# A fourth couple of FFN chunks by seven block products, in three of four FFN stages of a decoder trunk

## The chip, the cores and the metric

The kernel runs on 1 core of a Trainium2 chip. The metric is the time of one execution on the device in microseconds (us), the median of several. Every time below is in us unless it is marked ns. PE is TensorE, DVE is VectorE, ACT is ScalarE, POOL is GpSimd; SP issues the loads, and POOL issues those that add to what lies in the buffer.

## The reference

Two layers, each with an FFN, a mixer and a second FFN on 256 tokens of width 1024; the FFN has 2816 inner columns. So there are four FFN stages and two mixers, in the order FFN, mixer, FFN, FFN, mixer, FFN.

```python
def rms_norm(x, g):
    xf = x.astype(jnp.float32)
    y = xf * lax.rsqrt(jnp.mean(xf * xf, axis=-1, keepdims=True) + EPS)
    return (y * g.astype(jnp.float32)).astype(x.dtype)

def swiglu(h, wi, wo):
    gate, up = jnp.split(h @ wi, 2, axis=-1)
    return (jax.nn.silu(gate) * up) @ wo
...
    for l in range(DEPTH):
        h = rms_norm(x, ffn1_pre_g[l])
        x = x + 0.5 * rms_norm(swiglu(h, ffn1_wi[l], ffn1_wo[l]), ffn1_post_g[l])
        h = rms_norm(x, mix_pre_g[l])
        y = hybrid_mixer(h, w_in[l], a_ln_g[l], a_ln_b[l], a_ws[l], a_bs[l],
                         w_pa[l], w_pb[l], w_pc[l], w_o[l])
        x = x + rms_norm(y, mix_post_g[l])
        h = rms_norm(x, ffn2_pre_g[l])
        x = x + 0.5 * rms_norm(swiglu(h, ffn2_wi[l], ffn2_wo[l]), ffn2_post_g[l])
```

The mixer is not touched by the change.

## The kernel before, in words

**Tiles.** The 256 tokens are two tiles of 128. The inner columns are 11 chunks of 256 (numbered 0 to 10), each with its gate and its up columns, so that one chunk's first product is 512 columns wide. Weights are fp32 and are worked on in two parts: `hi`, a cast by ACT (L231), and `lo`, what the cast left over, by a subtraction on DVE (L232). The tokens are split in the same way (`hh`, `hl`). Each product is three matmuls (`mm3`, L391 to L395: hi by hi, hi by lo, lo by hi). A chunk's first product for one token tile is eight steps over the width 1024, so 24 matmuls of 512 columns.

**Weights.** They come in units of 1 MB. A generator (`loader`, from L161) issues the loads in a fixed order, `plan` (from L127), on SP's queue: a wait of one load holds all that stand behind it. A unit goes into one of two buffers `raw`; `splitter` (from L223) makes hi and lo of each half unit, into rings of eight, or into buffers with the tag `q4` (nine of 128x1024) for units named in `place`. The `q4` buffers are shared with the mixer's large tiles, with the token sums, with `wa` and `wb` below, and, in a stage that follows a mixer, with the halves of chunk 0's units.

**Couples of chunks.** `QUADS = (4, 6, 8)`: chunks 4 and 5, 6 and 7, 8 and 9 are taken in couples by `pair7` (from L525), which makes the 2 by 2 blocks (two chunks, two token tiles, the width in two halves) by seven block products instead of eight (12 matmuls each). For that it needs token sums, four tiles `s1` to `s4` for the whole stage (`sums`, L487 to L514: twelve operations of 128x512 on DVE, four casts on ACT), and weight sums for each couple. Those are `wa`, `wb` and `wf`: DVE makes `wf` by L240 and L245, and POOL issues loads that add to what is in `wb` (L184) and in `wa` (L241). In the plan a couple is `B11`, `T2`, a wo unit, `B21`, `T3`, `T1`, a wo unit, `T4`, `B22`; the names stand for the weight blocks and sums in the order in which they are split. Of a couple's results, `u2` and `u3` are kept (L545) and added to or subtracted from later ones.

**Order in a stage.** Chunks 0 and 1 come first for both token tiles: in the first FFN tile by tile for each chunk, in the other three (0, tile 0), (1, tile 0), (0, tile 1), (1, tile 1). Then `sums` starts; chunks 2 and 3 are taken in the plain way, each after a unit of the second weight `wo` (products `acc`); then come the three couples, and chunk 10. The stage's start overlaps the end of the stage before: the norm of the second token tile (`prenorm`, from L344: two squares on ACT, `rs` on POOL, `xn` on DVE, transposes on PE) is worked out while PE does the first tile's products.

**Who sets the order.** The program is emitted by coroutines along a clock of estimates (`Clock`), and a list scheduler then sets the order of each engine's instructions; operations marked `high_priority` come earlier. Each engine works through its own list in order. What the scheduler made of both programs is shown with the change.

Of the kernel before, what the change touches and what calls it, by code (L numbers as in the profile page):

```python
# [24 lines left out]
EPS = 1e-6  # L25
NEG = -1.0e30
UNITS = 106
QUADS = (4, 6, 8)

NOSYNC = mybir.DependencyInfo(mybir.DependencyClass.NoSync, mybir.DependencyReason.DATA)  # L30
HOT = 60
# [7 lines left out]

class Flag:  # L40
    on = False


class Clock:
# [33 lines left out]
def trunk(ctx, tc, x, wpk, gains, lnp, wst, bst, consts, out, depth=DEPTH):  # L78
    nc = tc.nc
    V, S, G, T = nc.vector, nc.scalar, nc.gpsimd, nc.tensor  # L80
    ck = Clock()
# [44 lines left out]

    plan = []  # L127
    for l in range(depth):
        for st0, qj in ((0, QUADS), (33, None), (73, QUADS)):
            b = UNITS * l + st0  # L130
            if qj is None:
                plan += [("w", b + i) for i in range(40)]
                continue

            def c(j, q):
                return b + (2 * j if j < 2 else 3 * j - 1 if j < NCH - 1 else 28) + q

            def w(j):
                return b + (4 + 3 * j if j < NCH - 3 else j + 22)

            plan += [("w", c(j, q)) for j in range(2) for q in range(2)]
            for j in range(2, NCH - 1, 2):
                if j in qj:
                    k = Quad({}, c(j, 0), c(j, 1), c(j + 1, 0), c(j + 1, 1))
                    if j != qj[0]:
                        k.ffn, k.prev, last.next, k.par = last.ffn, last, k, 1 - last.par
                    else:
                        k.prev, k.par = None, 0
                    k.next = None
                    last = k  # L150
                    plan += [("B11", k), ("T2", k), ("w", w(j - 2)), ("B21", k), ("T3", k), ("T1", k),
                             ("w", w(j - 1)), ("T4", k), ("B22", k)]
                else:
                    for i in (j, j + 1):
                        plan += [("w", w(i - 2)), ("w", c(i, 0)), ("w", c(i, 1))]
            plan += [("w", c(NCH - 1, q)) for q in range(2)] + [("w", w(NCH - 3 + i)) for i in range(3)]
    NI = len(plan)
    WQ = (slice(0, 1024), slice(1024, 2048))
    done, raw = set(), {}

    def loader():  # L161

# [45 lines left out]
    def ready(n, kind, k):  # L208
        if kind[0] == "T":
            raw[n] = k.b if kind == "T3" else k.ffn["a" if kind == "T1" else "f"]  # L210
        return n in raw

    def splitter():
        for n, (kind, k) in enumerate(plan):
            while not ready(n, kind, k):
                next(ld)
            halves[n] = []
            for q in range(2):
                gate = place.get(n)
                while st_["free"] <= 0 if gate is None else not gate.on:  # L220
                    yield 0.2
                    gate = place.get(n)
                if gate is not None:  # L223
                    h = sp.tile([P, 1024], F32R, tag="q4", name=f"hi{n}_{q}", bufs=9)
                    lo = sp.tile([P, 1024], F32R, tag="q4", name=f"lo{n}_{q}", bufs=9)
                else:
                    st_["free"] -= 1
                    h = rp.tile([P, 1024], F32R, tag="hi", name=f"hi{n}_{q}", bufs=RING)
                    lo = rp.tile([P, 1024], F32R, tag="lo", name=f"lo{n}_{q}", bufs=RING)
                r = raw[n][q]  # L230
                S.copy(h, r)  # L231
                V.tensor_sub(lo, r, f32(h))  # L232
                halves[n].append((h, lo))
                yield 1.2
            if kind == "B11":
                f = k.ffn
                if "f" not in f:
                    f["f"] = [sp.tile([P, 1024], F32, tag="xn", name=nm("wf"), bufs=2) for _ in WQ]
                for q, c in enumerate(WQ):
                    V.tensor_add(f["f"][q], f["a"][q], k.b[q])  # L240
                    nc.gpsimd.dma_start(f["a"][q], wpk[k.u12][:, c], accum_op=ALU.add)  # L241
                    yield 0.6
            elif kind == "B21":
                for q in range(2):
                    V.tensor_add(k.ffn["f"][q], k.ffn["f"][q], raw[n][q])  # L245
                    yield 0.6
            elif kind == "T1":
                k.t1 = True
            done.add(n)
            for _ in range(3):  # L250
                next(ld, None)
# [92 lines left out]
    def prenorm(tt, gi, flag, st=None):  # L344

        xn = sp.tile([P, DM], F32, tag="xn", name=nm("xn"), bufs=2)
        st = sp.tile([P, 2], F32, tag="ss", name=nm("ss"), bufs=4)
        for i, h in enumerate(HF):
            with tc.high_priority(offset=HOT):
                q = S.activation(xn[:, h], xs[tt][:, h], AF.Square, scale=DM ** -0.5, accum_out=st[:, i:i + 1])  # L350
                if gi == 0 and tt == 1:
                    tc.add_manual_dep(q.ins, lasthi[0].ins.name, NOSYNC, reason="first tile first")
            if i == 0:
                yield 0.6
        r = rstd_of(st[:, 0:1], st[:, 1:2])
        yield 1.7
        gn = gain(gi)
        with tc.high_priority(offset=HOT):
            for h in HF:
                V.scalar_tensor_tensor(xn[:, h], xs[tt][:, h], r, gn[:, h], op0=ALU.mult, op1=ALU.mult)  # L360
        yield 1.0
        for i, h in enumerate(HF):
            to_T(xn[:, h], tt, 4 * i, 4, hh, hl)
            yield 0.7
        flag.on = True

    def post_half(acc, yn, st, i, gi, mul):

# [62 lines left out]
        ck.tick()  # L431


    def ffn(gi, nxt, first):
        acc = [None, None]
        gT, gf = {}, {}
        always = Flag()
        always.on = True
        for i in (32 + 3 * len(QUADS), 33 + 3 * len(QUADS)):
            place[st_["pos"] + i] = always  # L440

        def wi(us, j, tt, rel):
# [82 lines left out]
        def pair7(j, ss):  # L525
# [26 lines left out]
            def chunk(jj, tt, a, b, op):  # L552
# [24 lines left out]
        ss = []  # L577
        ua, ub = take(2), take(2)
        order = ((ua, 0, 0), (ua, 0, 1), (ub, 1, 0), (ub, 1, 1)) if first else \
                ((ua, 0, 0), (ub, 1, 0), (ua, 0, 1), (ub, 1, 1))  # L580
        for w, j, tt in order:
            wi(w, j, tt, tt == 1)
        ck.start(sums(ss), 0.2)
        for j in range(2, NCH - 1):
            if j == 4:
                if first:
                    load_consts()
                gain(gi + 1)
                gain(gi + 2)
            if j // 2 * 2 in QUADS:  # L590
                if j % 2 == 0:
                    pair7(j, ss)
                continue
            uo = take(1)[0]
            wo(uo, j - 2, 0, False)
            wo(uo, j - 2, 1, True)
            us = take(2)
            wi(us, j, 0, False)
            wi(us, j, 1, True)
# [334 lines left out]
        T.matmul(warm[:, 0:P], ident, ident, start=True, stop=True)  # L934
    for l in range(depth):
        b = 6 * l
        ffn(b, b + 2, l == 0)
        mixer(l, b + 2, b + 4)
        ffn(b + 4, b + 6 if l + 1 < depth else None, False)
    while ck.ev:  # L940
        ck.until(lambda: not ck.ev)

# [96 lines left out]
```

## Time and profile before

| what | us |
|---|---|
| median of 3 runs | 1259.87 (1258.27 to 1259.88) |
| the profiled execution's own time | 1260.91 |
| its span in the profile | 1259.2 |
| PE busy in it | 1240.5 (99%) |
| DVE busy | 949.3 (75%) |
| ACT busy | 729.5 (58%) |
| POOL busy | 75.5 (6%) |

By the products on PE the second FFN stage goes from 456.5 to 637.3, the third from 637.3 to 818, the fourth from 1074.5 to 1252.6. The stage in which the change is followed here is the second: chunks 0 and 1 from 456.5 to 480.9, chunks 2 and 3 with two wo units to about 514.6, and three couples of about 31 us each to 607.

A line of the trace's timeline gives start, duration, engine, source line, operation, the tile written and the tiles read, and in brackets how long the engine sat idle before it and what it waited for. DVE's and PE's durations overlap with the next instruction; the distance of two starts is what an instruction takes in a row of such.

### The profile page before, as it was taken

What the parts mean: (1) busy time and instruction counts of PE and PEld (TensorE: products, weight loads), DVE (VectorE), ACT (ScalarE), POOL (GpSimd) and SP (SyncE); (2) the same over time, 40 slices, a digit from 0 to 9 for tenths busy, and PEclk for the clock granted to TensorE, in tenths of its full rate; (3) what the DMA queues carried; (4) which work ended last, traced back from release to release, by engine and by line L of the source; (5) the groups of instructions that cost most, each with busy time, mean ns of one, the idle gap of its engine ahead of it and who ended that gap; (6) DMA issues with size and microseconds to landing.
All of it is one profiled execution on the core that took longest, in us unless ns stands there. A gap on an engine that the chain in (4) does not pass through costs nothing.

```text
span 1259.2 us, 16367 instructions
## 1 busy us (share of the span) xinstructions
PE 1240.5 (99%) x6284; PEld 1029.3 (82%) x6284; DVE 949.3 (75%) x1185; ACT 729.5 (58%) x996; POOL 75.5 (6%) x129
## 2 busy tenths in 40 slices
PE   8999999999999999999999999999999999999997
PEld 6777878998778878888878888789977788888886
DVE  5889977645765877899768899865467668689983
ACT  5566656435656465666645666654366655557652
POOL 0001001000000010010011010010000000110000
PEclk8999999999999999999999999999999999999999
DMA  7899555554435557885668785744543455687851
GB/s 251 279 316 264 172 201 194 188 212 166 136 134 178 192 167 271 261 270 167 239 207 260 252 258 185 236 175 161 210 181 119 149 173 200 213 240 250 250 195 65
DMA packets 45294, 259.41 MB, mean 206 GB/s; under 512 B 5280, under 2 KB 5408, under 8 KB 21280
## 3 DMA queue, kind: packets, MB, share of 16 engines
q1 hardware_dynamic: 38304, 233.20, 52.0%
q0 software_dynamic: 6912, 25.17, 10.5%
q8 instruction: 49, 0.80, 0.3%
q14 instruction: 29, 0.24, 0.1%
HBM read 257.30 MB, written 1.05 MB: 205 GB/s over the span
## 4 chain that ended last, share of the span: by engine, by line
PE 82%; DMA 6%; DVE 6%; ACT 3%; issue 1%; POOL 1%; SPq 0%; DVEq 0%; POOLq 0%; ACTq 0%
PE mm L392 15%; PE mm L394 15%; PE mm L393 15%; DMA raw<-wpk 5%; PE acc L394 5%; PE acc L393 5%; PE acc L392 5%; DVE lo L232 3%; PE qk L393 3%; PE qk L394 3%; PE qk L392 3%; PE tr L339 2%; ACT hi L231 2%; PE pj L394 1%; PE pj L392 1%; PE pj L393 1%
## 5 line engine op out<-in xcount | busy, mean ns | idle before, releaser
L232 DVE TENSOR_TENSOR lo<-raw,hi 128x1024 fp32r<-128x1024 f32 x376 | 451.8, 1220 | 153.2 <-ACT hi L231 148.1
L231 ACT CAST hi<-raw 128x1024 fp32r<-128x1024 f32 x376 | 387.2, 1050 | 259.4 <-DMA raw<-wpk 78.6
L392 PE MATMUL mm<-hi,hh 128*128 128x512 f32 x784 | 314.0, 401 | 1.7 <-ACT hh L332 1.7
L394 PE MATMUL mm<-hi,hl 128*128 128x512 f32 x784 | 307.3, 392 | 0.2 <-DVE hl L333 0.2
L393 PE MATMUL mm<-lo,hh 128*128 128x512 f32 x784 | 306.8, 391 | 0.0
L392 PEld LDWEIGHTS mm<-hi,hh 128*128 128x128 f32 x784 | 147.9, 189 | 33.3 <-issue 2.7
L394 PEld LDWEIGHTS mm<-hi,hl 128*128 128x128 f32 x784 | 147.7, 188 | 32.7 <-DVE hl L333 0.9
L393 PEld LDWEIGHTS mm<-lo,hh 128*128 128x128 f32 x784 | 148.1, 189 | 27.9
L392 PE MATMUL acc<-hi,gT 128*128 128x512 f32 x352 | 139.3, 396 | 0.2 <-ACT gT L332 0.2
L394 PE MATMUL acc<-hi,gT 128*128 128x512 f32 x352 | 137.6, 391 | 0.3 <-DVE gT L333 0.3
L393 PE MATMUL acc<-lo,gT 128*128 128x512 f32 x352 | 137.7, 391 | 0.0
L392 PE MATMUL qk<-hh,hi 128*128 128x256 f32 x320 | 91.2, 285 | 0.0
L394 PE MATMUL qk<-hh,lo 128*128 128x256 f32 x320 | 90.5, 283 | 0.0
L393 PE MATMUL qk<-hl,hi 128*128 128x256 f32 x320 | 90.5, 283 | 0.0
L392 PE MATMUL mm<-hi,sA 128*128 128x512 f32 x192 | 77.2, 402 | 0.8 <-DVE sg L479 0.8
L394 PEld LDWEIGHTS acc<-hi,gT 128*128 128x128 f32 x352 | 66.1, 188 | 14.3 <-DVE gT L333 0.8
L392 PEld LDWEIGHTS acc<-hi,gT 128*128 128x128 f32 x352 | 66.1, 188 | 13.5 <-ACT gT L332 0.7
L393 PEld LDWEIGHTS acc<-lo,gT 128*128 128x128 f32 x352 | 66.2, 188 | 13.0
L394 PE MATMUL mm<-hi,sA 128*128 128x512 f32 x192 | 75.1, 391 | 0.0
L393 PE MATMUL mm<-lo,sA 128*128 128x512 f32 x192 | 74.9, 390 | 0.0
L332 ACT CAST gT<-tr 128x256 fp32r<-128x256 f32 x88 | 32.5, 369 | 63.6 <-PE tr L339 63.5
L393 PEld LDWEIGHTS qk<-hl,hi 128*128 128x128 f32 x320 | 61.4, 192 | 0.1
(170 smaller groups left out, 1724.2 us busy)
## 6 DMA issues: line engine op xcount, KB each, us to landing
raw<-wpk SPq DMA_DIRECT2D x187, 1024.0 KB, 4.9
wb<-wpk SPq DMA_DIRECT2D x24, 512.0 KB, 7.0
wb<-wpk POOLq DMA_DIRECT2D x24, 512.0 KB, 9.2
wa<-wpk SPq DMA_DIRECT2D x24, 512.0 KB, 6.0
wa<-wpk POOLq DMA_DIRECT2D x24, 512.0 KB, 9.5
gain<-gains SPq DMA_DIRECT2D x12, 512.0 KB, 7.7
x<-x SPq DMA_DIRECT2D x2, 512.0 KB, 5.6
raw<-wpk SPq DMA_DIRECT2D x2, 512.0 KB, 6.5
```

The lines of the kernel that those rows point to most:

```text
L231: S.copy(h, r)
L232: V.tensor_sub(lo, r, f32(h))
L332: lasthi[0] = S.copy(h_out, src)
L339: T.transpose(tr[:, k * P:(k + 1) * P], src[:, k * P:(k + 1) * P], ident)
L392: T.matmul(o, ah, bh, start=first, stop=False, skip_group_check=go_on)
L393: T.matmul(o, ah, bl, start=False, stop=False, skip_group_check=go_on)
L394: T.matmul(o, al, bh, start=False, stop=stop, skip_group_check=go_on)
```

## The change

Chunks 2 and 3 become a fourth couple in the second, third and fourth FFN stage; the first stage keeps three. The parity of the `wb` buffers is counted from the last couple on, so that the new couple's second `wb` tile takes the tag `shl`. The first couple's B11 is split only once the second token tile's norm is emitted (`normed`). `sums` starts after the third of the four first products instead of after the fourth. The gains are loaded at chunk 3 instead of 4.

```diff
-QUADS = (4, 6, 8)
+FOUR = (1, 2, 3)
...
+def quads(i):
+
+    return (2, 4, 6, 8) if i in FOUR else (4, 6, 8)
...
-        for st0, qj in ((0, QUADS), (33, None), (73, QUADS)):
+        for st0, qj in ((0, quads(2 * l)), (33, None), (73, quads(2 * l + 1))):
...
+                    k.par, k.gate = qj[::-1].index(j) % 2, 2 * l + st0 // 73 if j == 2 else None
                     if j != qj[0]:
-                        k.ffn, k.prev, last.next, k.par = last.ffn, last, k, 1 - last.par
+                        k.ffn, k.prev, last.next = last.ffn, last, k
                     else:
-                        k.prev, k.par = None, 0
+                        k.prev = None
...
             if kind == "B11":
                 f = k.ffn
+                while k.gate is not None and k.gate not in normed:
+                    yield 0.2
...
         flag.on = True
+        if tt == 1:
+            normed.add({0: 0, 4: 1, 6: 2, 10: 3}.get(gi))
...
-    def ffn(gi, nxt, first):
+    def ffn(gi, nxt, idx):
+        first, qj = idx == 0, quads(idx)
...
-        for w, j, tt in order:
+        for i, (w, j, tt) in enumerate(order):
             wi(w, j, tt, tt == 1)
-        ck.start(sums(ss), 0.2)
+            if i == (3 if first else 2):
+                ck.start(sums(ss), 0.2)
         for j in range(2, NCH - 1):
-            if j == 4:
+            if j == (4 if first else 3):
...
-            if j // 2 * 2 in QUADS:
+            if j // 2 * 2 in qj:
```

PE's list has 5815 rows before and 5779 after the change: 36 rows fewer, which are 36 matmuls of 512 columns. The lists are the same up to the first mixer's end; from there they differ in the places shown.

SP's queue, around the start of the second FFN stage. raw73 to raw76 are the units of chunks 0 and 1, raw77 is the first wo unit in the new program and raw79 the unit B21; in the program before, raw77 is the first wo unit too, and raw78 and raw79 are chunk 2. Before:

```order
L115 DMA raw73_3729<-wpk 128x2048
L115 DMA raw74_3765<-wpk 128x2048
L115 DMA raw75_3794<-wpk 128x2048
L115 DMA raw76_3816<-wpk 128x2048
L115 DMA raw77_3877<-wpk 128x2048
L115 DMA raw78_3905<-wpk 128x2048
L115 DMA wb_307_3907<-wpk 128x1024
L115 DMA wb_308_3908<-wpk 128x1024
L115 DMA raw79_3952<-wpk 128x2048
L115 DMA raw80_3986<-wpk 128x2048
```

With the change:

```order
L120 DMA wb_289_3666<-wpk 128x1024
L120 DMA wb_290_3667<-wpk 128x1024
L120 DMA raw73_3735<-wpk 128x2048
L120 DMA raw74_3771<-wpk 128x2048
L120 DMA raw75_3800<-wpk 128x2048
L120 DMA raw76_3822<-wpk 128x2048
L120 DMA wa_299_3824<-wpk 128x1024
L120 DMA wa_300_3825<-wpk 128x1024
L120 DMA raw77_3887<-wpk 128x2048
L120 DMA raw79_3915<-wpk 128x2048
L120 DMA wb_311_3917<-wpk 128x1024
L120 DMA wb_312_3918<-wpk 128x1024
```

`wb`, the weights to which POOL adds, is loaded ahead of the four units of chunks 0 and 1; the two loads of `wa` stand behind these, and raw77 behind `wa`. POOL's list moves in the same way: its two accumulating loads of `wb` stood between the two norms' `rs`, and stand ahead of all four now.

DVE, second FFN stage, from the transposed result of chunk 0's first tile on (`gT`, `sg` are the results of chunks; `sA` are the token sums). Before:

```order
L333 TENSOR_TENSOR gT_320_4007<-tr_325_4049,gT_320_4007 128x256
L452 TENSOR_TENSOR sg_328_4062<-mm_321_4008,sg_328_4062 128x256
L333 TENSOR_TENSOR gT_326_4057<-tr_329_4077,gT_326_4057 128x256
L452 TENSOR_TENSOR sg_331_4095<-mm_327_4058,sg_331_4095 128x256
L232 TENSOR_TENSOR lo88_0_4105<-raw79_3952,hi88_0_4104 128x1024
L232 TENSOR_TENSOR lo88_1_4120<-raw79_3952,hi88_1_4119 128x1024
L333 TENSOR_TENSOR gT_320_4007<-tr_332_4114,gT_320_4007 128x256
L491 TENSOR_TENSOR sA_336_4146<-hh_94,hl_95 128x512
L232 TENSOR_TENSOR lo89_0_4132<-raw80_3986,hi89_0_4131 128x1024
L452 TENSOR_TENSOR sg_335_4143<-mm_330_4091,sg_335_4143 128x256
L491 TENSOR_TENSOR sA_337_4148<-hh_94,hl_95 128x512
L232 TENSOR_TENSOR lo89_1_4151<-raw80_3986,hi89_1_4150 128x1024
```

With the change:

```order
L341 TENSOR_TENSOR gT_324_4005<-tr_329_4047,gT_324_4005 128x256
L463 TENSOR_TENSOR sg_334_4066<-mm_325_4006,sg_334_4066 128x256
L341 TENSOR_TENSOR gT_332_4061<-tr_335_4089,gT_332_4061 128x256
L248 TENSOR_TENSOR wf_330_4052<-wa_299_3824,wb_289_3666 128x1024
L238 TENSOR_TENSOR lo86_0_3924<-wa_299_3824,hi86_0_3923 128x1024
L248 TENSOR_TENSOR wf_331_4053<-wa_300_3825,wb_290_3667 128x1024
L238 TENSOR_TENSOR lo86_1_3943<-wa_300_3825,hi86_1_3942 128x1024
L238 TENSOR_TENSOR lo87_0_4070<-wf_330_4052,hi87_0_4069 128x1024
L238 TENSOR_TENSOR lo87_1_4080<-wf_331_4053,hi87_1_4079 128x1024
L463 TENSOR_TENSOR sg_337_4107<-mm_333_4062,sg_337_4107 128x256
L502 TENSOR_TENSOR sA_338_4110<-hh_94,hl_95 128x512
L502 TENSOR_TENSOR sA_339_4112<-hh_94,hl_95 128x512
```

Before, the product `sg` of chunk 0's second tile (mm_327) stood right behind the first tile's `gT`; now six operations of 128x1024 on `wa` and `wb` stand ahead of that product (mm_333 here), and the first token sums behind it.

PE, second FFN stage, where chunk 1's second tile ends (mm_336) and the first couple begins (mm_350), with the change:

```order
L402 MATMUL mm_336_4103<-hi85_1_3903,hh_94 128x512
L403 MATMUL mm_336_4103<-lo85_1_3904,hh_94 128x512
L404 MATMUL mm_336_4103<-hi85_1_3903,hl_95 128x512
L402 MATMUL acc_352_4231<-hi88_0_4120,gT_324_4005 128x512
L402 MATMUL acc_353_4232<-hi88_0_4120,gT_324_4005 128x512
L347 MATMUL tr_342_4136<-ident_73,sg_337_4107 128x128 x2
L402 MATMUL mm_350_4191<-hi86_0_3923,hh_94 128x512
L403 MATMUL mm_350_4191<-lo86_0_3924,hh_94 128x512
```

The transposes of that `sg` (tr_342) stand two matmuls behind the last product of chunk 1.

PE, where T3's product ends (into mm_351 or mm_368) and T1's begins, with the change: first in the new couple, then in the next one:

```order
L403 MATMUL mm_351_4192<-lo90_1_4214,sA_345_4173 128x512
L404 MATMUL mm_351_4192<-hi90_1_4213,sA_345_4173 128x512
L402 MATMUL mm_358_4316<-hi91_0_4223,sA_340_4128 128x512
...
L402 MATMUL mm_368_4449<-hi99_1_4496,sA_345_4173 128x512
L403 MATMUL mm_368_4449<-lo99_1_4497,sA_345_4173 128x512
L404 MATMUL mm_368_4449<-hi99_1_4496,sA_345_4173 128x512
L402 MATMUL acc_352_4231<-hi101_0_4535,gT_361_4350 128x512
L402 MATMUL acc_353_4232<-hi101_0_4535,gT_361_4350 128x512
L402 MATMUL acc_354_4251<-hi101_0_4535,gT_361_4350 128x512
L402 MATMUL acc_355_4252<-hi101_0_4535,gT_361_4350 128x512
L402 MATMUL mm_373_4589<-hi100_0_4507,sA_340_4128 128x512
```

The tile into which T1 goes (mm_358, mm_373) takes the PSUM buffer of T3's, which DVE's `u3` reads (L556 now, L545 before). Before, T1's product followed T3's directly as well, into the buffer of an earlier product, which DVE had read (L479) before.

## Rows read from the trace of the kernel before

**Rows 1.** The page, busy time of each engine over the span (share of the span, instructions).

```profile
PE 1240.5 (99%) x6284; PEld 1029.3 (82%) x6284; DVE 949.3 (75%) x1185; ACT 729.5 (58%) x996; POOL 75.5 (6%) x129
```

**Rows 2.** Windows, one middle couple of the second FFN stage; busy us, instructions, PEclk, DMA share, GB/s.

```profile
545.00:575.90 30.90, 30.90 (x141) 25.38 (x140) 30.60 (x37) 21.73 (x28) 2.59 (x3) 1.00 0.87 256
```

**Rows 3.** Timeline of PE, the stage's first wo product, and the next product, both ends.

```profile
480.71 0.39 PE L392 MATMUL acc<-hi,gT 128*128 128x512 f32 x1
486.39 0.39 PE L392 MATMUL mm<-hi,hh 128*128 128x512 f32 x1
...
494.78 0.39 PE L393 MATMUL mm<-lo,hh 128*128 128x512 f32 x1
```

**Rows 4.** Chain of waits, second FFN stage, the second token tile's norm.

```profile
462.51 0.95 POOL wb L184
464.52 0.76 DVE xn L360
465.42 0.63 PE tr L339 x4
```

**Rows 5.** Timeline of SP's queue, starts of the second and the fourth FFN stage.

```profile
456.11 14.87 SPq L115 DMA_DIRECT2D wb<-wpk  x2
1073.29 14.88 SPq L115 DMA_DIRECT2D wb<-wpk  x2
```

**Rows 6.** DMA, the load issued at 470.66 (the second wb): KB, us to landing.

```profile
wb<-wpk SPq DMA_DIRECT2D x1, 512.0 KB, 4.6
```

**Rows 7.** Timeline of DVE, second FFN stage.

```profile
473.57 0.42 DVE L333 TENSOR_TENSOR gT<-tr,gT 128x256 fp32r<-128x256 f32 x1 [3.16 <-ACT gT L332]
475.70 0.42 DVE L452 TENSOR_TENSOR sg<-mm,sg 128x256 f32<-128x256 f32 x1 [1.70 <-ACT sg L451]
...
481.53 0.68 DVE L491 TENSOR_TENSOR sA<-hh,hl 128x512 f32<-128x512 f32 x1
482.13 1.22 DVE L232 TENSOR_TENSOR lo<-raw,hi 128x1024 fp32r<-128x1024 f32 x1
483.26 0.42 DVE L452 TENSOR_TENSOR sg<-mm,sg 128x256 f32<-128x256 f32 x1
483.60 0.68 DVE L491 TENSOR_TENSOR sA<-hh,hl 128x512 f32<-128x512 f32 x1
...
501.30 1.21 DVE L240 TENSOR_TENSOR wf<-wa,wb 128x1024 f32<-128x1024 f32 x1
502.43 0.41 DVE L333 TENSOR_TENSOR gT<-tr,gT 128x256 fp32r<-128x256 f32 x1
```

**Rows 8.** Page and DMA: a 1 MB load's landing, all; then those issued at 72.8, 106.5.

```profile
raw<-wpk SPq DMA_DIRECT2D x187, 1024.0 KB, 4.9
raw<-wpk SPq DMA_DIRECT2D x1, 1024.0 KB, 8.5
raw<-wpk SPq DMA_DIRECT2D x1, 1024.0 KB, 11.0
```

**Rows 9.** Timelines of ACT and PE, third FFN stage, the second token tile's norm.

```profile
640.10 1.05 ACT L231 CAST hi<-raw 128x1024 fp32r<-128x1024 f32 x1
642.51 0.63 ACT L350 ACTIVATE xn<-x 128x512 f32<-128x512 f32 x1 [1.36 <-DVE x L382]
646.02 0.63 PE L339 MATMUL tr<-ident,xn 128*128 128x128 f32 x4 [0.44 <-DVE xn L360]
```

**Rows 10.** Timelines of PE and DVE, a block product's last matmul and its reader.

```profile
533.65 0.39 PE L394 MATMUL mm<-hi,sA 128*128 128x512 f32 x1
534.08 0.69 DVE L545 TENSOR_TENSOR cc<-mm,u 128x512 f32<-128x512 f32 x1
```

**Rows 11.** Timeline of PE and windows, the program's start.

```profile
10.66 0.79 PE L392 MATMUL mm<-hi,hh 128*128 128x512 f32 x1 [1.66 <-ACT hh L332]
10.00:14.00 4.00, 3.18 (x7) 2.08 (x8) 3.12 (x5) 3.52 (x9) 0.88 (x2) 0.50 0.88 303
18.00:20.00 2.00, 2.00 (x10) 1.65 (x9) 1.55 (x3) 1.98 (x4) 0.00 (x0) 1.00 0.82 254
```

More of the change, by code (lines that the diff above doesn't have):

```diff
@@ L158, in trunk @@
     WQ = (slice(0, 1024), slice(1024, 2048))
-    done, raw = set(), {}
+    done, raw, normed = set(), {}, set()
     def loader():
@@ L438, in ffn @@
         always.on = True
-        for i in (32 + 3 * len(QUADS), 33 + 3 * len(QUADS)):
+        for i in (32 + 3 * len(qj), 33 + 3 * len(qj)):
             place[st_["pos"] + i] = always
@@ L936, in trunk @@
         b = 6 * l
-        ffn(b, b + 2, l == 0)
+        ffn(b, b + 2, 2 * l)
         mixer(l, b + 2, b + 4)
-        ffn(b + 4, b + 6 if l + 1 < depth else None, False)
+        ffn(b + 4, b + 6 if l + 1 < depth else None, 2 * l + 1)
     while ck.ev:
```

## The prediction

> **What bounds the kernel now.** I read the page's busy times first: PE is busy 99% of the span, DVE 75% [rows 1], so the sum of PE's matmuls is the time, and a matmul less is a gain only while nothing else ends last. Next the windows by stage: in a middle couple DVE is busy 30.60 of 30.90 [rows 2]; PE and DVE are nearly equal there, and DVE keeps up only because it comes to a couple ahead of PE. Next PE's timeline for the price of a matmul: from 486.39 to 494.78 there are 37 starts [rows 3], 0.2268 each. Last the chain of waits and the queues at the start of a stage, where the change moves the most: PE waits there for the second tile's norm [rows 4], and a load of wb waits at the head of SP's queue [rows 5]. DVE idles in that place, 3.16 and 1.70 ahead of two results [rows 7]: it is the time in which DVE could work ahead, and the question is whether the change can use it.
>
> **What the change removes.** Two plain chunks for two tiles are 4 x 24 = 96 matmuls, a couple is 7 x 12 = 84. Twelve fewer in three stages are 36, as the order has it: 36 x 0.2268 = **8.2**. In the second stage POOL's issue of an accumulating load (0.95, at 462.51) lies in the chain to the second tile's norm, and PE's transposes wait at 465.42 [rows 4]. It now stands ahead of the norms. PE's next start came about 0.7 late there; I take **0.7** off (0 to 0.7), once only: in the fourth stage PE did not wait at that place. The gains' loads, moved by one chunk, have one answer, nothing: they wait at no engine in the rows that I read.
>
> **What it adds on DVE.** A couple splits 18 half units and adds wf four times, 22 operations of 128x1024, where two plain chunks have 12. Rates on DVE, by starts in a row: 128x1024 1.13 (482.13 to 483.26, 501.30 to 502.43), 128x512 0.60, 128x256 0.34 [rows 7]. The question is when they run.
>
> *The first couple, after a mixer (second and fourth stage).* All times here are the trace's own; what moves PE moves them together. The first load of wa needs the q4 buffer for which the second wb waited: SP stood at it from 456.11 on, and it was issued at 470.66, when PE had used chunk 0's first half for the second tile [rows 5, 6]. It landed after 4.6 [rows 6]; so wa is there at 475.3. In DVE's new order six operations on wa and wf stand ahead of sg of the second tile: 6 x 1.13 + 0.42 = 7.2, so sg is ready at 482.5. PE wants it for its transposes at about 481.3, two matmuls behind the last of chunk 1 (480.71 was the first wo matmul [rows 3]). From there to the last split that T2's product needs, by the order, DVE has five operations of 128x1024, eight of 128x512 and three of 128x256: 5.7 + 4.8 + 1.0 = 11.5, which is 494.0. PE has 44 matmuls and two couples of transposes (0.23 each) from 480.71 to T2: 10.5, so it would be there at 491.2. T2's last matmul is 17 starts on, at 497.9, and u2, which reads its product, can start 0.43 later (a reader started so long after its product's last matmul [rows 10]). After u2 (0.6) DVE has four operations of 128x1024, one of 128x512 and u3: 4.5 + 0.6 + 0.7, so u3 is done at 504.7. T1's product waits for u3, since it goes into the buffer that u3 reads. From 480.71 to T1 PE has 76 matmuls and the two couples of transposes: 17.2 + 0.5 = 17.7, so it would be there at 498.4. It waits **6.3** in all, in two or three pieces; without the wait of DVE for T2, 4.9. DVE does not use the idle time of 470 to 475: nothing in its order ahead of wa can run there, and the sums, which could, stand behind.
>
> *The next wo unit.* Its load is issued when lo of the first one is split, at about 487.5 (482.5 and five of DVE's operations more), behind accumulations that POOL issues from 477.6 on (as lo of wa's first half is done). PE wants its cast (1.05 [rows 9]) six matmuls into T2, at 495.4, so a landing up to 6.8 after the issue costs nothing. A 1 MB load lands after 4.9 in the median; two that were issued with accumulations under way took 8.5 and 11.0 [rows 8], which would cost 1.7 and 4.2. I take half of the smaller, **0.8**, since part of the accumulations has landed by then. So 7.1 a stage, 14.2 for two; bounds 4.9 and 10.5 a stage if the order of DVE decides, and nothing if its idle time could be used.
>
> *The third stage* follows an FFN, and wa's buffers come free with the last products of the stage before; DVE has its six operations done before the second tile. But ACT's casts of wa now stand ahead of the square of the second tile (642.51), behind which the transposes at 646.02 already wait [rows 9]. A cast is 1.05 [rows 9]: 0 to 1.05, I take **0.55**.
>
> *u3 in every couple.* In all couples of these stages T1's product now waits for u3, before for an earlier read. DVE starts on a product 0.43 after its last matmul did (533.65 to 534.08 [rows 10]) and needs 0.68; PE has 0.23 and, by the order, four wo matmuls, 0.91, to fill it. With DVE free, that is even: 1.11 against 1.14. With one 128x1024 operation in the way it is 1.1 to 1.2 late, and DVE is busy 99% of such a couple [rows 2]. I take 0.2 for each of the ten couples not counted above (0 to 1.2): **2.0** (0 to 12).
>
> **The sum**: -8.2 - 0.7 + 14.2 + 0.55 + 2.0 = +7.9. The profiled execution took 1260.91, 1.04 above the median of 1259.87; its time would become 1268.8, and against the median I forecast **1267.5**. A measurement of this kernel can tell about 0.2%, 2.5, from no change.
>
> **A rule against the change.** At the program's start PE sat 1.66 without work before 10.66, after only transposes, and the granted clock from 10 to 14 was 0.50, the lower of the two levels (1.2 GHz); it was back at 1.00 from 18 on [rows 11]. Waits of PE inside stages, such as that at 465.42, left it at 1.00. The Trainium skill (TensorE: Matmul & The Clock Gate, "HAM oscillation — how this bites in real kernels") says that PE's idle gaps between matmuls throttle the clock again; if the new waits came in long pieces, the clock would fall in them. My sum holds it at 1.00; the time with a fall, from rows, is rival 4's 1273.5.
>
> **The rivals.**
> 1. *DVE's work is done ahead* (faster). If wa landed 6 earlier, or DVE came to its sums in its idle time, PE would not wait for u3, and 8.2 + 0.7 would remain: 1252 on the profiled time, 1251 against the median. For it: DVE is idle 23% of its time as a whole, and 3.16 and 1.70 just there [rows 7]. Against: each engine keeps its order, wa's load waits on PE, and the point at which this decides is that DVE, which has u3 ready 29.4 after wa lands, would have to have it ready within the 23.1 from 475.3 to PE's arrival at 498.4. Chance 0.2, with the cases in which part of it holds.
> 2. *It evens out* (same). The waits of the first couple come at their lower bound (4.9 twice), because DVE loses nothing on T2 and the wo unit lands in time, and the later couples and the third stage cost nothing: -8.9 + 9.8 = +0.9, 1261 against the median. For it: T1's price is even with DVE free. Against: three things must all go well. Chance 0.15.
> 3. *DVE paces all couples* (much slower). One 128x1024 operation stands ahead of u3 in most of the ten couples, at 1.2 each, which adds up to 10 to the forecast: 1277. For it: 30.60 of 30.90 [rows 2], and no lead left after the first couple. Against: the order often has u3 placed early. Chance 0.12.
> 4. *The clock falls* in the waits of the second and fourth stage. At the lower level, seen from 10 to beyond 14, PE loses half of its work; six at that level cost 3, twice 6 in all: 1273.5. Against: 1.00 in all later waits. Chance 0.08.
> That the change does not do what it says is left out: the order has 36 rows fewer.
>
> **How the numbers follow.** My forecast has 0.45, with a range of its own of 1263 (the first couple's lower bound with the other terms) to 1273 (its upper bound in one stage and half of it in the other). Slower by over 0.2% is that with rivals 3 and 4: 0.65; same is rival 2, 0.15; faster is rival 1, 0.2. The whole range reaches from 1253, inside rival 1's lesser forms, to 1275; it leaves out about half of rival 1 and of rival 3, 0.16.
>
> **What would show it.** PE has 36 matmuls fewer. SP's loads of wa start at about 470, their casts at 475; sg of the second tile on DVE at about 482, u3 at 503 to 506, and PE's waits from 481 to 506 and in the fourth stage's like place name DVE's sums, sg and u, or ACT's hi, 4.9 to 10.5 together. The wait at 465 is gone. In the later couples PE waits at T1 for DVE's u (L556). It is wrong if PE waits for under 2 in the first couple, if DVE's idle time around 473 shrinks to nothing, or if the later couples take 30.9 or less each.

## The result, and the profile after

The changed kernel takes **1311.07** in the median of 5 runs (1304.79 to 1313.52), the kernel before 1259.87 on the same chip; the ratio is 1.0392, 95% interval 1.0364 to 1.0420. So it is slower by 49 to 51, where the forecast was 7.6. The profiled execution is the fastest of the five: 1304.79, span 1303.1, which is 43.9 above the span before.

The page of the changed kernel, busy times (as [rows 1]) and the DMA queues (q0 carries POOL's accumulating loads; its row before stands last; columns: packets, MB, share of the 16 DMA engines' span):

```profile
PE 1247.8 (96%) x6248; PEld 1024.3 (79%) x6248; DVE 990.0 (76%) x1230; ACT 738.6 (57%) x1017; POOL 84.6 (6%) x141
...
q1 hardware_dynamic: 39168, 233.20, 49.7%
q0 software_dynamic: 8640, 31.46, 13.1%
...
q0 software_dynamic: 6912, 25.17, 10.5%
```

PE has its 36 matmuls fewer (6248 against 6284), but more time passes in them. q0 has grown from 25.17 MB to 31.46 MB. What PE waited for, in the changed kernel (engine and line that waited, what for: us in total, times, longest):

```profile
PE tr L347 <- DVE xn L368: 13.5, 7, 3.6
PE tr L347 <- DVE cc L490: 9.7, 9, 2.2
PE acc L402 <- ACT hi L237: 9.0, 5, 3.7
PE tr L347 <- DVE sg L463: 4.5, 6, 1.2
PE mm L402 <- DVE u L556: 3.5, 4, 1.4
```

Before, the first of these was 3.3, the second 0.5, and there was no row for `acc` behind `hi` or for `u`. The largest wait is one that I had priced as a gain: the norm (`xn`). The chain of waits of the changed kernel at the end of the first mixer, where the first token tile of the second FFN stage is normed:

```profile
435.15 9.57 DMA raw<-wpk
444.80 1.06 ACT hi L237
445.88 2.36 DVE lo L238 x2
448.24 0.66 DVE yn L383 x2
...
453.90 0.76 DVE xn L368
454.80 0.72 PE tr L347 x4
455.52 0.43 PE wo L402
```

A 1 MB load takes 9.57. Behind it, on ACT and DVE, stand the operations of the norm, in the order of each engine; PE waits 3.63 for its transposes at 454.80, and the matmul after that takes 0.43 and not 0.23. POOL's timeline shows what ran beside that load: the two accumulating loads of the new couple's `wb`, moved to this place by the change.

```profile
430.92 0.95 POOL L190 DMA_DIRECT2D wb<-wpk  x1 [82.16 <-PE pj L404]
432.22 0.86 POOL L190 DMA_DIRECT2D wb<-wpk  x1 [0.35 <-issue]
```

The first couple of the second stage, in DVE's timeline and PE's (what answers to [rows 7] and [rows 3]):

```profile
477.59 1.23 DVE L248 TENSOR_TENSOR wf<-wa,wb 128x1024 f32<-128x1024 f32 x1 [0.78 <-DMA wa<-wpk]
...
484.41 0.42 DVE L463 TENSOR_TENSOR sg<-mm,sg 128x256 f32<-128x256 f32 x1
...
504.45 0.69 DVE L556 TENSOR_TENSOR u<-mm,u 128x512 f32<-128x512 f32 x1 [4.85 <-PE mm L404]
...
510.20 0.68 DVE L556 TENSOR_TENSOR u<-mm,u 128x512 f32<-128x512 f32 x1
```

```profile
500.02 1.22 PE L402 MATMUL acc<-hi,gT 128*128 128x512 f32 x2 [3.33 <-ACT hi L237]
501.04 0.63 PE L404 MATMUL mm<-hi,sA 128*128 128x512 f32 x1
...
510.94 0.50 PE L402 MATMUL mm<-hi,sA 128*128 128x512 f32 x1 [1.45 <-DVE u L556]
```

sg is done 7.2 after the start of wf, as worked out. At 500.02 PE waits for the next wo unit's cast; that load was issued at 489.90 and took 8.9. DVE, whose next operation is u2, waits 4.85 for T2's product. Then u2, u3 and T1 follow, T1 0.06 after u3's end.

Windows of the changed kernel (columns as [rows 2]): behind the two waits of over 3 in the second stage, then behind a wait of 2.21 at 745.32 in the third, then the second and third couple of the second stage:

```profile
454.80:458.00 3.20, 3.20 (x11) 2.52 (x12) 3.20 (x4) 0.86 (x2) 0.00 (x0) 0.56 0.00 0
500.60:503.00 2.40, 2.40 (x7) 1.90 (x6) 0.00 (x0) 0.61 (x3) 0.00 (x0) 0.50 0.93 386
745.30:748.70 3.40, 3.38 (x9) 2.81 (x10) 3.32 (x5) 0.79 (x2) 0.00 (x0) 0.51 0.94 378
518.60:550.40 31.80, 31.23 (x142) 25.45 (x141) 28.79 (x33) 20.31 (x27) 3.43 (x4) 1.00 0.95 298
550.40:585.00 34.60, 31.55 (x142) 25.34 (x141) 31.88 (x37) 20.76 (x28) 3.47 (x4) 1.00 0.82 243
```

The granted clock is at or near 0.50, the lower of its two levels, in the first three; so it is in a fourth place, from 1144.7 to 1148.1, behind a wait of 3.73. Behind the waits of 2.62 at 667.94 and 2.35 at 1101.11 it stayed at 1.00. A couple that took 30.9 [rows 2] takes 31.8 and 34.6. In the longer one the chain of waits goes through a 1 MB load again (9.09), the casts, DVE's splits and `cc`, to the transposes of PE:

```profile
536.96 9.09 DMA raw<-wpk
...
550.36 0.27 ACT gT L340
550.64 0.42 DVE gT L341
551.07 3.40 DVE lo L238 x3
554.47 0.34 DVE cc L490
```

Last the third stage's start, ACT's timeline (as [rows 9]):

```profile
661.84 1.04 ACT L237 CAST hi<-wa 128x1024 fp32r<-128x1024 f32 x1
663.20 1.05 ACT L237 CAST hi<-wa 128x1024 fp32r<-128x1024 f32 x1 [0.32 <-DMA wa<-wpk]
664.15 0.63 ACT L358 ACTIVATE xn<-x 128x512 f32<-128x512 f32 x1
```

The casts of wa do stand ahead of the square, as forecast, and the second waits for its load to land. Before the changed kernel reaches this point it has lost time to a 1 MB load that took 10.0, issued at 638.65 beside two accumulations at 636.96 and 638.18.

### The profile page after: what moved, and what is told of

Read it like the earlier page. It is cut to its first block, busy times and chain, and to the rows that moved or that the text cites. A ratio compares the mean times of both kernels' runs of the same rounds, so it can differ in the third digit from the quotient of the medians.

```text
span 1303.1 us, 16449 instructions
## 1 busy us (share of the span) xinstructions
PE 1247.8 (96%) x6248; PEld 1024.3 (79%) x6248; DVE 990.0 (76%) x1230; ACT 738.6 (57%) x1017; POOL 84.6 (6%) x141
## 3 DMA queue, kind: packets, MB, share of 16 engines
q0 software_dynamic: 8640, 31.46, 13.1%
HBM read 263.59 MB, written 1.05 MB: 203 GB/s over the span
## 4 chain that ended last, share of the span: by engine, by line
PE 58%; DVE 16%; DMA 14%; ACT 8%; issue 3%; POOL 1%; SPq 0%; ACTq 0%; DVEq 0%; POOLq 0%
PE mm L402 10%; PE mm L404 10%; PE mm L403 10%; DMA raw<-wpk 10%; DVE lo L238 10%; ACT hi L237 6%; DMA wa<-wpk 3%; PE qk L402 3%; PE qk L404 3%; PE qk L403 3%; PE acc L402 3%; PE acc L404 2%; PE acc L403 2%; PE tr L347 2%; PE pj L404 1%
## 5 line engine op out<-in xcount | busy, mean ns | idle before, releaser
L238 DVE TENSOR_TENSOR lo<-raw,hi 128x1024 fp32r<-128x1024 f32 x364 | 435.7, 1222 | 131.7 <-ACT hi L237 128.3
L237 ACT CAST hi<-raw 128x1024 fp32r<-128x1024 f32 x364 | 370.7, 1048 | 265.3 <-DMA raw<-wpk 118.1
L402 PE MATMUL mm<-hi,hh 128*128 128x512 f32 x724 | 290.2, 401 | 1.6 <-ACT hh L340 1.6
L403 PE MATMUL mm<-lo,hh 128*128 128x512 f32 x724 | 285.0, 394 | 0.0
L404 PE MATMUL mm<-hi,hl 128*128 128x512 f32 x724 | 284.7, 393 | 0.2 <-DVE hl L341 0.2
L402 PEld LDWEIGHTS mm<-hi,hh 128*128 128x128 f32 x724 | 136.6, 189 | 31.8 <-issue 2.7
L403 PEld LDWEIGHTS mm<-lo,hh 128*128 128x128 f32 x724 | 136.9, 189 | 25.3
L402 PE MATMUL mm<-hi,sA 128*128 128x512 f32 x240 | 96.9, 404 | 4.4 <-DVE u L556 3.5
L403 PE MATMUL mm<-lo,sA 128*128 128x512 f32 x240 | 95.1, 396 | 1.4 <-DVE lo L238 1.3
L404 PE MATMUL mm<-hi,sA 128*128 128x512 f32 x240 | 95.1, 396 | 0.0
L340 ACT CAST gT<-tr 128x256 fp32r<-128x256 f32 x88 | 32.3, 367 | 80.1 <-PE tr L347 79.8
L237 ACT CAST hi<-wa 128x1024 fp32r<-128x1024 f32 x60 | 62.6, 1051 | 22.1 <-DMA wa<-wpk 14.3
## 6 DMA issues: line engine op xcount, KB each, us to landing
wb<-wpk POOLq DMA_DIRECT2D x30, 512.0 KB, 10.5
```

Source lines behind the costliest of these rows:

```text
L340: lasthi[0] = S.copy(h_out, src)
L402: T.matmul(o, ah, bh, start=first, stop=False, skip_group_check=go_on)
L403: T.matmul(o, ah, bl, start=False, stop=False, skip_group_check=go_on)
L404: T.matmul(o, al, bh, start=False, stop=stop, skip_group_check=go_on)
```

## The experiments

Two theories. **L**: 1 MB loads land late behind POOL's accumulating loads, which the change adds and puts where the norm of the next stage, the first couple and couples without a lead depend on the loads; the clock falls in the waits. **D**: DVE's own order (wa, wf and the sums ahead of what PE wants) is most of it, as the prediction had it. Ratios are to the kernel before, run on the same chip between the others; 0.0100 is 12.6.

**e1, the sums alone.**

```diff
-FOUR = (1, 2, 3)
+FOUR = ()
```

> Three couples in every stage; of the change only the earlier token sums and the earlier gains remain. Theory L (1 MB loads that land late behind POOL's accumulating loads, at the stages' starts and in couples without a lead, are most of the loss) expects about the time before, 1258 to 1263. Theory D (DVE's own order, with wa, wf and the sums ahead of what PE wants, is most of the loss) expects the same, since the six operations on wa and wf are gone from that place; over 1265 would mean that the sums' new place costs by itself.

Measured: 1259.01, ratio 1.0004 (0.9992 to 1.0017). The earlier sums and gains cost and give nothing; all that is lost comes with the fourth couple.

**e2, the third stage alone.**

```diff
-FOUR = (1, 2, 3)
+FOUR = (2,)
```

> The fourth couple in the third stage alone. Theory L: the stage's start loses about 8 and the later couples 1 to 3 each, 2.7 are saved: 1267 to 1274. Theory D: DVE has its six operations done early in this stage, so the time is 1257 to 1262.

Measured: 1271.40, ratio 1.0100 (1.0082 to 1.0118). This stage has DVE's six operations done early, and the couple costs 12.6 all the same. That is theory L's range. PE's longest wait in the stage, 3.33 at 726.57 ahead of the transposes of `cc`, ends a chain that begins with a 1 MB load of 10.34, issued at 707.41 while accumulations issued at 697.94 and 699.17 and two loads of gains were under way.

**e3, without the first couple's accumulations into wb.**

```diff
-            for q, c in enumerate(WQ):
+            for q, c in enumerate(WQ if k.gate is None else ()):
                 nc.gpsimd.dma_start(k.b[q], wpk[k.u22][:, c], accum_op=ALU.add)
```

> The changed kernel without the two accumulating loads into wb of each new couple (its wb holds one weight block instead of a sum of two; the output is not the reference's). Theory L: the 1 MB loads at the two mixers' ends and at the third stage's start land after 5 to 7 instead of 9.6 and 10.0, PE's waits of 3.8 and 2.5 there and the fall of the clock behind them go: 11 to 14 less, 1296 to 1301. Theory D: DVE's order is the same, 1308 or more.

Measured: 1294.98, ratio 1.0283 (1.0262 to 1.0305), just below theory L's range. Six accumulating loads of 0.5 MB less give 0.0109, some 14. The load at the mixer's end, by the DMA view of the changed kernel (issued at 435.15):

```profile
raw<-wpk SPq DMA_DIRECT2D x1, 1024.0 KB, 9.6
```

and of e3 (issued at 433.04):

```profile
raw<-wpk SPq DMA_DIRECT2D x1, 1024.0 KB, 4.8
```

**e4, without any accumulation in the second to fourth stage**, and **e5, the same with three couples.** e4's edit takes the two `dma_start` with `accum_op` out of these stages (L190, L249); e5 has `FOUR = ()` too.

> The changed kernel without any accumulating load in the second to fourth stage (wa and wb hold single weight blocks there; the output is not the reference's); all of DVE's, ACT's and PE's operations stay. Theory L: the late loads are gone everywhere, 1265 to 1283. Theory D: 1300 or more, since DVE has as much to do in the same order.

> Three couples in every stage (as e1) without accumulating loads in the second to fourth stage (wa and wb hold single weight blocks there; the output is not the reference's). It is to e4 what the kernel before is to the changed one. Theory L: with three couples the loads are early enough, so leaving the accumulations out gains little, 1252 to 1260; e4's 1271 is then 12 to 18 above it, and that part is DVE's order and not the loads. If the loads were all of the loss, this would be 1279 (e4 plus the 8.2 of PE's work).

Measured: e4 1271.32, ratio 1.0098 (1.0080 to 1.0116); e5 1258.42, ratio 0.9985 (0.9975 to 0.9994). The four together:

| ratio to the kernel before | with accumulations | without |
|---|---|---|
| three couples | 1 | 0.9985 |
| four couples | 1.0392 | 1.0098 |

With three couples the accumulations cost 2, with four 37 (0.0294). With three, the loads beside them have slack. Without any, the fourth couple still costs 14 (0.0113), although it saves 8.2 on PE: some 22 are lost again, of another cause. The list of PE's waits, 22 in sum in e4 and 9 in e5, names 13 of them. What PE waits for in e4:

```profile
PE tr L349 <- DVE xn L370: 6.7, 5, 2.6
PE mm L404 <- DVE u L558: 3.5, 4, 1.4
PE tr L349 <- DVE sg L465: 3.3, 4, 1.2
PE tr L349 <- DVE cc L492: 1.7, 4, 0.7
```

No `acc` behind `hi` is left, and `cc` fell from 9.7 to 1.7; no wait at the mixers' ends either. What stays is the first couple's chain on DVE (sg, u) and the second tile's norm in the third stage (2.6 for one).

A rival is that the buffers to which POOL adds come late themselves, and not the 1 MB loads beside them. ACT's waits for loads, in the changed kernel and then in e4:

```profile
ACT hi L237 <- DMA raw<-wpk: 118.1, 64, 6.3
ACT hi L237 <- DMA wa<-wpk: 14.3, 12, 2.3
...
ACT hi L238 <- DMA raw<-wpk: 85.2, 60, 3.7
ACT hi L238 <- DMA wa<-wpk: 20.3, 18, 2.4
```

Without accumulations ACT waits 33 less for 1 MB loads and no less for `wa`, and in neither list is there a wait of ACT or DVE for `wb`. What comes late is the 1 MB loads.

**e6, the first couple's wb four units earlier.**

```diff
-            if n + 4 < NI and plan[n + 4][0] == "B11" and not plan[n + 4][1].prev:
-                load_b(plan[n + 4][1])
+            if n + 4 < NI and plan[n + 4][0] == "B11" and not plan[n + 4][1].prev and plan[n + 4][1].gate is None:
+                load_b(plan[n + 4][1])
+            if n + 8 < NI and plan[n + 8][0] == "B11" and plan[n + 8][1].gate is not None:
+                load_b(plan[n + 8][1])
```

> The first couple's wb, with its accumulations, is loaded eight instead of four units ahead, so that the accumulations lie some 20 us earlier, away from the norm of the stage's first token tile. Theory L: the waits of 3.8 and 2.5 at the mixers' ends go, and part of the third stage's, if the loads that are late now have more slack there: 1298 to 1306; if they have as little, 1308 to 1315. Theory D: no change, 1308 to 1314.

Measured: 1312.53, ratio 1.0414 (1.0392 to 1.0435). The wait at the first mixer's end is gone, but two others came: the mixer's own transposes at 427, and a wo unit at the end of the second FFN stage, at 630:

```profile
PE acc L404 <- ACT hi L239: 16.7, 9, 5.3
...
PE tr L349 <- DVE mg L919: 2.4, 2, 1.2
```

So moving the accumulations moves the loss; here, too, the loads have little slack.

**e7, T1's product into the first product's PSUM tile.**

```diff
-            b0 = mm()
             prod(b0, *s1, take(1)[0], True)
```

> T1's product goes into the PSUM tile of the couple's first product again (as the kernel before had it), so that it waits for DVE's read of that tile and not for u3. The four waits of PE for u (3.5 in sum in the profile) go, and T1 can start up to 1.2 earlier in couples where DVE is late: 1304 to 1311 if the waits only move on to the next thing that is late (theory L), 1297 to 1303 if u3 paced the couples.

Measured: 1305.80, ratio 1.0356 (1.0341 to 1.0372), with intervals that touch the changed kernel's. (The edit holds for the first stage's couples too.) It is worth 0 to 10, about 5, in the changed kernel, and no more than a part. PE still waits for u (3.9 in 5 waits): now the product that comes next, into the other tile.

**e8, the next couple's wb later.**

```diff
-                if kind == "B21" and k.next:
+                if kind == "B22" and k.next:
                     load_b(k.next)
```

> The next couple's wb, with its accumulations, is loaded behind the unit B22 instead of behind B21, so that the next wo unit's load has only wa's accumulations beside it. Theory L: this load, 8.9 in the first couple of the changed kernel, lands after 5 to 7, PE's waits of 3.5 and 3.9 and the fall of the clock behind them go, and the later couples lose less: 1293 to 1303. Against it, wb comes later for the next couple: if that decides, 1308 or more. Theory D: 1308 to 1314.

Measured: 1314.24, ratio 1.0415 (1.0387 to 1.0443): a miss for the gain that theory L had listed first, and the case that it had named against it. The wait of 3.33 at the wo unit is gone, but now the later couples are late, by a wait that the changed kernel does not have (first line). And the edit holds for the first stage as well, which the change leaves alone: up to 455 PE waits there for casts as it does not in the changed kernel (second line), and the second stage's first transposes come at 461.85 and not at 454.80 (third line):

```profile
PE mm L402 <- DVE cc L556: 9.4, 6, 3.6
...
PE mm L402 <- ACT hi L237: 5.2, 2, 2.7
...
461.85 0.41 PE L347 MATMUL tr<-ident,xn 128*128 128x128 f32 x2 [2.93 <-DVE xn L368]
```

From these to the third stage's first transposes, in the two profiled executions, e8 takes 185.9 (to 647.78), the changed kernel 192.6 (to 647.38). So in the second stage the move gained 6.7, and it lost 7.1 before it and 2.9 in the fourth. The total does not speak against theory L; the move in the three new stages alone was not tried.

**e9, three couples, with wb's accumulations where the change puts them.** The kernel of e1, with the first couple's `load_b` ten units ahead and its second buffer taken from the tag `shl` (as the change has it):

```diff
-            if n + 4 < NI and plan[n + 4][0] == "B11" and not plan[n + 4][1].prev:
-                load_b(plan[n + 4][1])
+            for d in (4, 10):
+                if n + d < NI and plan[n + d][0] == "B11" and not plan[n + d][1].prev and (d == 10) == (n > 40):
+                    load_b(plan[n + d][1])
...
-                    k.par, k.gate = qj[::-1].index(j) % 2,
+                    k.par, k.gate = (qj[::-1].index(j) + (l + st0 > 0)) % 2,
```

> Three couples in every stage (as e1), but the first couple's wb in the second to fourth stage, with its two accumulating loads, stands where the change puts it, ahead of the units of chunks 0 and 1. DVE, ACT and PE have the work of the kernel before. Theory L: the first token tile's norm is late at the two mixers' ends (4.5 and 2.5 in the changed kernel, the clock's fall with it), the third stage's start loses 3 or more: 1266 to 1273. Theory D: 1257 to 1263.

Measured: 1274.00, ratio 1.0110 (1.0083 to 1.0136), just above theory L's range. No matmul and no operation of DVE is added, only the place of wb's loads and accumulations (six each) and one buffer's tag are changed: 13 more than e1. PE's largest waits in e9 are for the norm, and the clock falls behind those at the two mixers' ends (the waits, then windows):

```profile
PE tr L348 <- DVE xn L369: 10.7, 4, 3.4
```

```profile
455.00:459.00 4.00, 3.99 (x13) 3.31 (x14) 3.40 (x4) 1.17 (x3) 0.00 (x0) 0.50 0.78 260
1082.80:1086.00 3.20, 3.20 (x11) 2.68 (x12) 3.20 (x4) 0.79 (x2) 0.00 (x0) 0.57 0.69 289
```

That fits e3: 14 less there when these accumulations are taken away, 13 more here when they, and the plain loads of wb ahead of them, are moved to that place.

**e10, plain loads from POOL in place of the accumulating ones.**

```diff
-                nc.gpsimd.dma_start(k.b[q], wpk[k.u22][:, c], accum_op=ALU.add)
+                nc.gpsimd.dma_start(k.b[q], wpk[k.u22][:, c])
```

(in the second to fourth stage, and in the same way for wa)

> The changed kernel with plain loads in place of the accumulating ones in the second to fourth stage: same issuer, same bytes, same waits, but the buffer is overwritten and not added to (the output is not the reference's). If adding is what keeps the 1 MB loads beside them late (in the page, accumulating loads hold 10.5% of the DMA engines' time for 25.2 MB, other loads 52.0% for 233.2, so 1.9 times as much for a byte): 1275 to 1292, between e4 and the changed kernel. If a second queue with that many bytes does it whatever it carries: 1303 or more.

Measured: 1283.04, ratio 1.0194 (1.0168 to 1.0220). That lies between: of the 0.0294 that the accumulations cost, 0.0198 go with the adding and 0.0096 stay with the same bytes in plain loads. The queue's row on e10's page and the landing of POOL's loads of wb, then the changed kernel's:

```profile
q0 software_dynamic: 8640, 31.46, 8.3%
...
wb<-wpk POOLq DMA_DIRECT2D x30, 512.0 KB, 7.2
...
wb<-wpk POOLq DMA_DIRECT2D x30, 512.0 KB, 10.5
```

The same 31.46 MB hold the DMA engines for 8.3% of the span with 25.17 MB of them as plain loads (the first stage's 6.29 MB still add), and for 13.1% with the adding throughout. The load at the first mixer's end took 8.4 beside the two plain loads, 9.57 beside the adding ones, 4.8 beside none (e3): at that one place the bytes do most of it.

**e11, e4 with e7's edit**, and **e12, e4 with the split of B11 after all four first products** (`normed.add(idx)` behind the fourth `wi` in `ffn`, and not in `prenorm`).

> e4 (no accumulating loads) with T1's product in the PSUM tile of the couple's first product. Of e4's 1271 the waits of PE for u are 3.5 in sum: 1266 to 1269 if T1's wait for u3 is a cost by itself (4.9 to 6.3 a stage in the prediction), 1270 to 1273 if DVE is so late in the first couple that the wait only moves to the next split.

> e4 with the first couple's B11 split only after all four first products are emitted: DVE's order then has sg and most token sums ahead of the splits of wf, of wa's second half and of the next wo unit. The DVE work up to u3 is the same, and wa's first half still stands ahead of sg, so DVE's idle time before wa stays unused. If the sum of DVE's work after wa's landing sets the end: 1269 to 1273. If the order within it does: 1262 to 1267.

Measured: e11 1274.27, ratio 1.0122 (1.0099 to 1.0146), just above its range; e12 1270.81, ratio 1.0093 (1.0078 to 1.0109). Neither differs from e4 beyond the noise. Neither another tile for T1's product nor another place for sg and the sums among DVE's operations gains anything by itself. The names of the waits change: PE waits 5.4 in 4 waits for the casts of wo units in e12, where it waited 3.5 in 4 for u in e4. That fits the total of DVE's work from wa's landing on, for the second and the fourth stage; it was not shown by a kernel with less of that work.

Of the twelve kernels none beats the one before, beyond e5, which leaves work out. A version that keeps the loads in time and needs no accumulations at the mixers' ends was not found; a third `raw` buffer, or a buffer for a plain second load and an add on an idle engine, was not tried.

## Why the prediction was right or wrong

The sign was right, the size was not: 7.6 forecast, 49 to 51 measured, outside the range of 1253 to 1275. The sign was not luck: without accumulations (e4) the fourth couple still costs 12. (A slip in the sum: 1268.8 less 1.04 is 1267.8, not 1267.5; and the lower bound of 4.9 for the first couple stands without its working.) Step by step:

- **What is removed: 36 matmuls, 8.2.** Right in count (6248 rows against 6284); in the time it does not show, since even without accumulations more than that is lost elsewhere.
- **POOL's load "now stands ahead of the norms", 0.7 off.** This is the step that failed. I followed the moved instruction on POOL's list, where it gives 0.7 back, and not on the DMA engines, where it delays the 1 MB loads beside it. The wait at 465 is gone as forecast, and 3.63 at 454.80, 2.35 at 1101.11 and the late loads of the third stage's start came in its place. e3 and e9 put it at 13 to 14. I had the price in hand: 8.5 and 11.0 for loads beside accumulations [rows 8], and used it for one load only, the next wo unit. The loads beside all other accumulations, in the later couples above all, stood at nothing in the sum; those accumulations cost 23 more (e3 to e4).
- **The first couple, 7.1 a stage (4.9 to 10.5).** The total was right, its parts were not, and that two errors nearly cancel is luck. PE's waits from 484 to 511 are 1.12 + 3.50 + 0.49 + 0.91 + 1.61 = 7.6 against the usual distance of starts (8.0 in the fourth stage, in the same places), and the clock's fall behind the second comes on top. The names are as forecast: sg, the wo unit's cast, DVE, u3. sg came 7.2 after wf began. But the wo unit, which landed after 8.9 (I took 7.6, within rows 8), cost 3.50 where I took 0.8, and the rest is 4.1 where I took 6.3: T2's product did not wait for DVE's splits, DVE waited 4.85 for that product. Without accumulations (e4) the waits are 1.14 + 0.49 + 0.91 + 1.61 = 4.2.
- **The third stage, 0.55 (0 to 1.05).** The mechanism was right (wa's casts ahead of the square), the size was not. I priced the casts and not the landing for which they wait (663.17). With the late loads before it, PE's waits there are 1.04, 0.66, 0.99, 2.77 and 0.60, together 6.1. In e4 the norm's 2.73 is still there, and the clock falls behind it (0.50 from 651.5 to 654.9). The stage alone costs 12.6 (e2), but not at this place: the second tile's transposes wait 0.78 there (0.44 before), and the longest wait comes in a later couple.
- **u3 in every couple, 2.0 (0 to 12).** Not borne out as a cause. The later couples of the second stage take 31.8, 34.6 and 32.3 and lose about 6 together, but in their chain stand loads of 9.09 and 8.48 and the transposes of `cc`, and without accumulations (e4) they take 31.4, 31.1 and 31.4. The four waits for u all lie in the first couples, not in the later ones as I had named them; e7 bounds T1's place at 0 to 10 in all, and without accumulations e11 finds nothing.
- **Rival 4, the clock.** It came with the waits, as named, and my sum, which held it at 1.00, was wrong. It fell in four places, behind waits of 3.63, 3.33, 2.21 and 3.73. By the mean clock, 0.990 against 0.996, 1303.1 x 0.010 - 1259.2 x 0.004 = 8 of PE's work are lost, the program's two ends included; the four stretches, 13.6 together at half the rate, are 6.8 of it. That the rival had 6 is luck: it had two long falls. The Trainium skill (TensorE: Matmul & The Clock Gate, "HAM oscillation — how this bites in real kernels") says that PE's idle gaps between matmuls throttle the clock again. Here the trace agrees, in the four places. But not every gap did it, and its length did not tell which: the clock stayed at 1.00 behind 2.62 at 667.94 and, in e12, behind 3.57 at 653.63.
- **Rivals 1 and 2** did not happen; **rival 3** had a loss in the later couples (1.2 each; 0.9, 3.7 and 1.4 measured in the second stage) and put it down to DVE alone. Some 5 of these 6 go with the accumulations (e4).

So of 49, the place of the first couple's accumulations is 14, the other accumulations 23 (e3 to e4, 0.0185), and 12 is what the couple costs beyond its saved matmuls without any of them. Part of each of the first two is the clock (0.990 in the changed kernel's profile, 0.994 in e3's, 0.996 in e4's). The cause of the 12 stays open in part: the waits have names, but no run took them away.

## What to carry to other kernels

When a transfer is moved, follow it on two lists: that of its issuer, and that of the loads that run beside it at the new place; then ask which of those has slack, and what stands behind it. A load's median landing says nothing of a place where another queue is at work: price it by the rows that had such company. Here PE and DVE were nearly equal in a couple, and 36 saved matmuls were worth nothing while DVE's work and the loads grew. And before an experiment is read, see which stages its edit reaches: e8's total hid a gain in one stage behind a loss in another.

## What was not expected of the hardware

- An accumulating load holds the DMA engines for longer than a plain one of the same bytes: 13.1% of the span for 31.46 MB, against 8.3% with 25.17 MB of it plain (e10), and a landing of 10.5 against 7.2 for wb. A 1 MB load beside two of them took 9.57 (8.4 beside two plain ones, e10; 4.8 without, e3).
- Some waits of PE are paid twice. Behind the 3.63 at 454.80 the matmuls ran at 0.43 instead of 0.23 until about 458. The same fall came behind a wait of 2.21, and not behind one of 3.57.
